# x's first piece loaded as two transfers of 64 rows instead of one of 128

## The chip, the core and the metric

The kernel runs on one core of a Trainium2 chip. The metric is device time in microseconds (us), the median of several runs. A profile is one execution of the same program, recorded by the chip's own profiler; its span goes from the first to the last recorded instruction, and is a little shorter than the device time.

The core has engines that run at the same time, each with its own instruction list: VectorE (DVE), ScalarE (ACT), GpSimd (POOL), TensorE (not used here) and SyncE (SP), which here only issues transfers and waits. Transfers between the chip's main memory (HBM) and the core's working memory (SBUF, 128 partitions) are carried by 16 DMA engines. SP and ACT can each issue transfers; each has its own queue, and both queues feed the same 16 DMA engines.

## What is computed

```python
def setup_inputs():
    batch, dim = 1024, 4096
    return {
        "x": np.random.randn(batch, dim).astype(np.float32),
        "y": np.random.randn(batch, dim).astype(np.float32),
    }

def reference(x: np.ndarray, y: np.ndarray) -> np.ndarray:
    z = x * y
    return (0.5 * z * (1 + np.tanh(np.sqrt(2 / np.pi) * (z + 0.044715 * z ** 3)))).astype(np.float32)
```

Two arrays of 16.78 MB are read, multiplied element by element, passed through the tanh form of GELU, and one array of 16.78 MB is written: 50.33 MB in all.

## The kernel before

Every element stands alone, so the kernel may lay the data out as it likes. It treats each array as flat, 32,768 elements for each of the 128 partitions, and cuts it into three pieces (`PIECES`, line 14). In the text they are called 0, 1 and 2:

- piece 0: columns 0 to 1,280; a row of one partition is 5,120 bytes, the whole piece 0.66 MB;
- piece 1: columns 1,280 to 17,664; a row is 65,536 bytes, the piece 8.39 MB;
- piece 2: columns 17,664 to 32,768; a row is 60,416 bytes, the piece 7.73 MB.

`columns` (line 51) makes the view of a piece: each partition's row is one contiguous run in HBM. All of x stays in SBUF (`xs`, line 61), and is overwritten by the product and then by the result. y has a smaller buffer (`ys`, line 62), parts of which are used twice. `Y_LOADS` (line 16) gives the order in which y's pieces are loaded and where in `ys` they go: piece 1, then piece 2, then piece 0. In the text these three transfers are y0, y1 and y2, the loads of x's pieces are x0, x1 and x2, and the stores, in the order of `STORES` (line 21), are those of piece 1, piece 2 and piece 0.

There is no scheduler: the program is written out by hand, and each engine works through its own list in order.

SP's list (lines 79 to 86 and 111 to 121): issue x0; take part in two barriers of all engines at the entry; wait until x0 has landed (line 81); issue y0 and x2; wait for three multiplies and issue y1; wait for the fourth and issue y2 (`Y_FREE`, line 18, gives these counts, since y1 and y2 reuse parts of y0's buffer); wait for y1's landing and issue the first store; wait for ACT and issue the second and the third store; wait until the stores have landed.

ACT's list: issue x1, the barriers, load the table of the GELU function, and then one ACTIVATE for each multiply as soon as that is done (lines 105 to 108).

DVE's list (lines 91 to 104): for each piece of y wait for the x piece with the same columns (lines 92 to 94) and for the y piece (line 95), then multiply in steps (`STEPS`, line 20): four of 4,096 columns, then seven of 2,048 and one of 768, then one of 1,280.

`_hoist` (line 25) takes instructions out of the place where they were written and puts them, in their order, ahead of their engine's first drain in the program's first block, that is, ahead of the entry barriers. Lines 79 and 80 do this with x0's issue on SP and x1's on ACT.

A transfer adds 16 to its semaphore in all, in single steps as the 16 DMA engines finish their share; so a wait for 16 is a wait until it has landed.

Of the kernel before, what the change touches and what calls it, by code (L numbers as in the profile page):

```python
# [1 line left out]

# [4 lines left out]


F32 = mybir.dt.float32
GELU = mybir.ActivationFunctionType.Gelu_apprx_tanh  # L10

PIECES = [(0, 1280), (1280, 17664), (17664, 32768)]

Y_LOADS = [(1280, 17664, 4056), (17664, 32768, 0), (0, 1280, 15104)]

Y_FREE = [0, 3, 4]

STEPS = [[4096] * 4, [2048] * 7 + [768], [1280]]  # L20
STORES = [(1280, 17664), (17664, 32768), (0, 1280)]
Y_BUF = 20440


def _hoist(nc, issued):

    here = nc.cur_bb.bb.instructions
    first = nc.main_func.blocks[0].instructions
    for ins in issued:
        del here[next(k for k, i in enumerate(here) if i is ins or i.name == ins.name)]  # L30
    engine = issued[0].engine
    at = next(
        k
        for k, i in enumerate(first)
        if i.engine == engine and type(i).__name__ == "InstDrain"
    )
    first[at:at] = issued


@with_exitstack  # L40
def kernel(
    ctx: ExitStack,
    tc: tile.TileContext,
    x: bass.AP,
    y: bass.AP,
    out: bass.AP,
):
    nc = tc.nc
    P = nc.NUM_PARTITIONS

    def columns(t, a, b):

        flat = t.flatten_outer_dims().rearrange("r c -> (r c)")
        pa, pb = next(q for q in PIECES if q[0] <= a and b <= q[1])
        return flat[P * pa : P * pb].rearrange("(p c) -> p c", p=P)[:, a - pa : b - pa]


    tc.close()
    tc.compile()  # L59

    xs = nc.alloc_sbuf_tensor("xs", [P, PIECES[-1][1]], F32).ap()
    ys = nc.alloc_sbuf_tensor("ys", [P, Y_BUF], F32).ap()
    sem_x = [nc.alloc_semaphore(f"sem_x{i}") for i in range(len(PIECES))]
    sem_y = [nc.alloc_semaphore(f"sem_y{i}") for i in range(len(Y_LOADS))]
    sem_mul = nc.alloc_semaphore("sem_mul")
    sem_act = nc.alloc_semaphore("sem_act")
    sem_o = [nc.alloc_semaphore(f"sem_o{i}") for i in range(len(STORES))]

    def load_x(i, engine=nc.sync):
        a, b = PIECES[i]  # L70
        return engine.dma_start(out=xs[:, a:b], in_=columns(x, a, b)).then_inc(sem_x[i], 16)

    def load_y(i):
        a, b, r = Y_LOADS[i]
        return nc.sync.dma_start(
            out=ys[:, r : r + b - a], in_=columns(y, a, b)
        ).then_inc(sem_y[i], 16)

    _hoist(nc, [load_x(0).ins])
    _hoist(nc, [load_x(1, nc.scalar).ins])  # L80
    nc.sync.wait_ge(sem_x[0], 16)
    load_y(0)
    load_x(2)
    for i in range(1, len(Y_LOADS)):
        if Y_FREE[i]:
            nc.sync.wait_ge(sem_mul, Y_FREE[i])
        load_y(i)

    n = 0
    done = {}  # L90
    for i, (a, b, r) in enumerate(Y_LOADS):
        for j, (xa, xb) in enumerate(PIECES):
            if xa <= a < xb:
                nc.vector.wait_ge(sem_x[j], 16)
        nc.vector.wait_ge(sem_y[i], 16)  # L95
        c = a
        for w in STEPS[i]:
            nc.vector.tensor_mul(  # L98
                out=xs[:, c : c + w],
                in0=xs[:, c : c + w],  # L100
                in1=ys[:, r + c - a : r + c - a + w],
            ).then_inc(sem_mul, 1)
            n += 1
            done[c + w] = n
            nc.scalar.wait_ge(sem_mul, n)
            nc.scalar.activation(  # L106
                out=xs[:, c : c + w], in_=xs[:, c : c + w], func=GELU
            ).then_inc(sem_act, 1)
            c += w

    for i, (a, b) in enumerate(STORES):
        if i == 0:
            nc.sync.wait_ge(sem_y[-2], 16)
        nc.sync.wait_ge(sem_act, done[b])
        nc.sync.dma_start(out=columns(out, a, b), in_=xs[:, a:b]).then_inc(sem_o[i], 16)
    for i in range(len(STORES) - 1):
        nc.sync.wait_ge(sem_o[i], 16)
    nums = sorted(s.num for s in [*sem_x, *sem_y, *sem_o[:-1], sem_mul, sem_act])
    assert nums == list(range(nums[0], nums[-1] + 1))
    nc.sync.sem_clear(range(nums[0], nums[-1] + 1))  # L120
    nc.sync.wait_ge(sem_o[-1], 16).then_inc(sem_o[-1], -16)


# [1 line left out]
_INS = ['x', 'y']  # L125
_OUTS = [((1024, 4096), 'float32')]


# [23 lines left out]
```

## Time and profile before

Three runs took 119.91, 119.82 and 119.84 us, a median of 119.84. The profiled execution's span is 118.52 us.

| from the profile before | us |
|---|---|
| device time, median of three runs | 119.84 |
| span of the profiled execution | 118.52 |
| x0 (on SP's queue): issued, landed | 0.00, 13.6 |
| x1 (on ACT's queue): issued, landed | 0.13, about 30.5 |
| y0: issued, landed | 13.57, 42.56 |
| x2: issued, landed | 13.96, about 60.4 |
| y1: issued, landed | 55.78, 78.25 |
| y2: issued, landed | 60.12, about 79.8 |
| store of piece 1: issued, landed | 78.27, about 98.7 |
| store of piece 2: issued | 96.55 |
| store of piece 0: issued, landed | 97.71, 118.5 |
| DVE busy in all, ACT busy in all | 35.2, 31.0 |

How to read it. "Issued" is the start of the issuing instruction on its engine, "landed" the time at which its semaphore was complete. A queue is worked off in order on each DMA engine, and a transfer issued behind another on the same queue starts only when the other's rows are done: x2's 46.5 us from issue to landing are mostly time behind y0. The trace also keeps a record for each packet that the DMA engines moved, with its start, duration and size, but without the number of the DMA engine; here a packet is one partition's row, and each transfer ends with one packet of 4 bytes on each DMA engine, its write to the semaphore. Where the text below gives times of rows or of semaphore writes, they are from these records. In the profile's lines SPq and ACTq stand for the issuing side of SP and ACT, and L71 is line 71 of the kernel.

### The profile page before, as it was taken

Reading aid. Unit: us, or ns where it says so; the run is one execution under the profiler, and the core shown is the slowest. Engines: PE = TensorE matmul, PEld = TensorE weight load, DVE = VectorE, ACT = ScalarE, POOL = GpSimd, SP = SyncE. Lnnn points to the kernel's source line nnn. Section 1 sums busy time; section 2 is a strip of 40 time slices with the busy share of each in tenths; the row PEclk is TensorE's granted clock in tenths of the full one; section 3 lists DMA queues with packets and bytes.
Section 4 is the critical chain, followed back from the end, with each engine's and each line's share of the span. In section 5 each row is a group of like instructions: output and inputs, shape, how many; then the busy total and the mean of one; then the engine's idle time right before and its main releaser. Section 6 shows DMA issues by size and latency. Waiting matters only on the chain.

```text
span 118.5 us, 82 instructions
## 1 busy us (share of the span) xinstructions
DVE 35.2 (30%) x13; ACT 31.0 (26%) x14; POOL 0.2 (0%) x4
## 2 busy tenths in 40 slices
DVE  0000000000000069999920000059999940000000
ACT  4000000000000000977975000006998990000000
POOL 0000000000000000000000000000000000000000
DMA  9888899889988897797797797798899887977975
GB/s 492 382 382 382 354 575 487 354 354 398 664 354 354 354 652 326 326 652 326 326 632 347 326 632 347 326 575 354 354 531 531 354 354 326 652 326 326 652 326 221
DMA packets 1296, 50.33 MB, mean 425 GB/s; under 512 B 144, under 2 KB 144, under 8 KB 528
## 3 DMA queue, kind: packets, MB, share of 16 engines
q1 hardware_dynamic: 1152, 41.94, 82.2%
q10 hardware_dynamic: 144, 8.39, 16.5%
HBM read 33.55 MB, written 16.78 MB: 425 GB/s over the span
## 4 chain that ended last, share of the span: by engine, by line
DMA 55%; DVE 24%; ACT 3%; issue 1%; DVEq 0%
DMA ys<-in_y_dram 43%; DVE xs L98 24%; DMA xs<-in_x_dram 11%; ACT xs L106 3%; DVEq L95 0%
## 5 line engine op out<-in xcount | busy, mean ns | idle before, releaser
L98 DVE TENSOR_TENSOR xs<-xs,ys 128x2048 f32<-128x2048 f32 (+3 forms) x13 | 35.2, 2777 | 60.9 <-DMA ys<-in_y_dram 60.9
L106 ACT ACTIVATE xs<-xs 128x2048 f32<-128x2048 f32 (+3 forms) x13 | 29.7, 2301 | 65.1 <-DVE xs L98 65.1
L106 ACT ACT_TABLE_LOAD x1 | 1.3, 1283 | 1.6 <-PEq L59 1.6
L136 POOL MEMSET const-bfloat16-1.0<- 128x1 bf16 x1 | 0.1, 103 | 0.0
L136 POOL MEMSET const-uint8-127<- 128x1 uint8 x1 | 0.1, 102 | 0.0
L136 POOL MEMSET const-float32-0.0<- 128x1 f32 x1 | 0.1, 100 | 0.2 <-issue 0.2
L136 POOL MEMSET const-float32-1.0<- 128x1 f32 x1 | 0.1, 99 | 0.0
## 6 DMA issues: line engine op xcount, KB each, us to landing
xs<-in_x_dram SPq DMA_DIRECT2D x1, 7552.0 KB, 46.5
ys<-in_y_dram SPq DMA_DIRECT2D x1, 7552.0 KB, 22.5
out_dram<-xs SPq DMA_DIRECT2D x1, 7552.0 KB, 20.4
xs<-in_x_dram SPq DMA_DIRECT2D x1, 640.0 KB, 13.6
ys<-in_y_dram SPq DMA_DIRECT2D x1, 640.0 KB, 19.7
out_dram<-xs SPq DMA_DIRECT2D x1, 640.0 KB, 20.8
xs<-in_x_dram ACTq DMA_DIRECT2D x1, 30.4
ys<-in_y_dram SPq DMA_DIRECT2D x1, 29.0
```

The costliest lines, as they stand in the source:

```text
L98: nc.vector.tensor_mul(out=xs[:, c : c + w], in0=xs[:, c : c + w], in1=ys[:, r + c - a : r + c - a + w],).then_inc(sem_mul, 1)
L106: nc.scalar.activation(out=xs[:, c : c + w], in_=xs[:, c : c + w], func=GELU).then_inc(sem_act, 1)
L136: nc = _bacc.Bacc("TRN2", target_bir_lowering=False, num_devices=1)
```

## The change

The load of x's piece 0 is made of two transfers, of partitions 0 to 63 and of partitions 64 to 127. Both are issued by SP, one behind the other, and both are hoisted ahead of the entry barriers, where the one transfer was. Each adds 16 to the same semaphore, so that the two places that wait for piece 0, SP ahead of y0's issue and DVE ahead of its last multiply, wait for 32. The bytes, their places in HBM and SBUF, and everything else stay as they were.

```diff
-    def load_x(i, engine=nc.sync):
+    def load_x(i, engine=nc.sync, p=slice(0, P)):
         a, b = PIECES[i]
-        return engine.dma_start(out=xs[:, a:b], in_=columns(x, a, b)).then_inc(sem_x[i], 16)
+        return engine.dma_start(out=xs[p, a:b], in_=columns(x, a, b)[p]).then_inc(sem_x[i], 16)
 
     def load_y(i):
...
-    _hoist(nc, [load_x(0).ins])
+    low, high = slice(0, P // 2), slice(P // 2, P)
+    _hoist(nc, [load_x(0, nc.sync, low).ins, load_x(0, nc.sync, high).ins])
     _hoist(nc, [load_x(1, nc.scalar).ins])
-    nc.sync.wait_ge(sem_x[0], 16)
+    nc.sync.wait_ge(sem_x[0], 32)
     load_y(0)
     load_x(2)
...
         for j, (xa, xb) in enumerate(PIECES):
             if xa <= a < xb:
-                nc.vector.wait_ge(sem_x[j], 16)
+                nc.vector.wait_ge(sem_x[j], 32 if j == 0 else 16)
         nc.vector.wait_ge(sem_y[i], 16)
```

## The prediction

> **What bounds the kernel now.** I began with the page of the profile: which engine is busy, and how evenly the transfers fill the span.
>
> ```profile
> span 118.5 us, 82 instructions
> DVE 35.2 (30%) x13; ACT 31.0 (26%) x14; POOL 0.2 (0%) x4
> DMA  9888899889988897797797797798899887977975
> DMA packets 1296, 50.33 MB, mean 425 GB/s; under 512 B 144, under 2 KB 144, under 8 KB 528
> q1 hardware_dynamic: 1152, 41.94, 82.2%
> q10 hardware_dynamic: 144, 8.39, 16.5%
> ```
>
> No compute engine works a third of the span, while the two DMA queues together hold the 16 DMA engines for 82.2 + 16.5 = 98.7% of it. Next, the table of stretches, to see where the missing 1.3% lies (columns: stretch, length, DVE, ACT, POOL, clock, DMA share, GB/s).
>
> ```profile
> 0.00:1.00 1.00, 0.00 (x0) 0.00 (x0) 0.20 (x4) 1.00 0.00 0
> 1.00:118.20 117.20, 35.20 (x13) 31.01 (x14) 0.00 (x0) 1.00 1.00 429
> 118.20:118.50 0.30, 0.00 (x0) 0.00 (x0) 0.00 (x0) 1.00 0.00 0
> ```
>
> It lies at the two ends. From 1.0 to 118.2 us the DMA share is 1.00: nothing can start earlier in the middle, so the end moves only with the work of the DMA engines, with a hole in their stream, or with its start. Then the timeline and SP's waits, for the order of the transfers.
>
> ```profile
> 0.00 0.38 SPq L71 DMA_DIRECT2D xs<-in_x_dram  x1
> 0.13 0.37 ACTq L71 DMA_DIRECT2D xs<-in_x_dram  x1
> ...
> 1.57 1.28 ACT L106 ACT_TABLE_LOAD   x1 [1.57 <-PEq L59]
> 13.57 0.34 SPq L75 DMA_DIRECT2D ys<-in_y_dram  x1
> 13.96 0.43 SPq L71 DMA_DIRECT2D xs<-in_x_dram  x1
> ```
>
> ```profile
> SPq L75 <- DMA xs<-in_x_dram: 12.0, 1, 12.0
> ```
>
> The 0.66 MB of x's first piece (x0) take until 13.57 us, because ACT's queue loads x1 beside it. In the packet records of the trace each DMA engine serves eight x0 rows (5,120 B, 196 ns), and from 2.3 us takes x1 rows (65,536 B, 2,418 ns) and x0's items in turn: five x0 rows before its first x1 row, then x1, row, x1, row, x1, row, x1, semaphore write. Check: 2.30 + 4 x 2.42 + 3 x 0.196 = 12.6 us; the semaphore writes stand at 12.66 to 13.19, and SP goes on 0.38 us after the last. x1's other four rows keep the engine busy until y0 arrives.
>
> **One engine's sum.** x0, y2 and the last store are 24 rows at 196 ns (4.7 us); x1 and the other two transfers of that width 24 rows at 2.42 us (58.1); the other three large ones 24 rows at 2.23 us (53.5): 116.3 us. The last engine starts its first row at 1.61 us, the first at 1.01; 1.61 + 116.3 = 117.9, against its last semaphore write at 118.11 and the end at 118.52. So the start of the last engine, and what its first rows lose, reach the end one for one. The median of the runs, 119.84, lies 1.32 us above this span; I add 1.32 to each span below.
>
> **The change, part by part.** *Second issue on SP.* One more instruction of 0.33 to 0.43 us (the issue rows of L75 and L71), at 0.38 us. Queued behind it: SP's part in the entry barriers. Its drain stands at 0.43 us, and the barrier passes when ACT's drain ends at 0.68; SP's now ends near 0.95, so the barriers pass some 0.3 us later, and with them the table load (1.57 to about 1.85). That is covered: the first ACTIVATE starts at 47.12 us, DVE waits for y0 until 42.66, SP for x0 until 13.57. Without cover it would cost 0.4 us. x1's issue is on ACT's own queue and is not moved.
>
> *Semaphores.* 16 more semaphore writes, one on each DMA engine, of 9 ns: 0.01 us. But each takes a turn against x1, so x0's ten items (4 rows, write, 4 rows, write) land at least one x1 packet, 2.4 us, later. The wait for 32 holds y0 and x2 back behind it on SP. The cover is x1: eight rows per engine. If n of the ten items are served before the first x1 row, the last write follows 10 - n x1 rows. With n = 5 (five fit before): 2.3 + 5 x 2.42 + 4 x 0.2 = 15.2 us. With n = 3: 2.3 + 7 x 2.42 + 5 x 0.39 = 21.2, some 21.7 on the last engine; y0's issue near 22.1 and its first packet 0.84 us later (the first large store: issued 78.27, first packet 79.11), 22.9, while the eighth x1 row still runs to 23.6. No hole, and y0's landing is set by bytes, not by its issue. DVE's wait for x0, at 94 us, has room to spare. What a later y0 would push: y1's issue at 55.78 waits for three multiplies behind y0, x2's transfer ends at 60.46; since a late stream delays both together, that margin stays.
>
> *64 rows instead of 128.* I take it that each half is still spread over all 16 engines, four rows each, as the 128 rows are; but it fills only half of SBUF's partitions at a time. The trace shows no such transfer, so bounds. Lower: rows keep their 196 ns, cost 0. A gain is possible at the start: the engines begin x0 spread over 0.60 us, and a list half as long may reach them in half the time, -0.3; at the very most all start with the first, -0.6. Upper: if two engines that fill the same half hold each other up so that together they move what one does, eight rows take 392 ns each: +8 x 0.196 = +1.57.
>
> Which end? Every long kind of packet runs at one rate per engine, 65,536 / 2,418 = 60,416 / 2,232 = 27.1 GB/s, loads and stores, beside rows of other transfers and without. That looks like a ceiling of the path into SBUF, not of HBM, and such a path can be shared. The nearest row of packets in one another's way is the first round: its 16 x1 rows, served while others still took x0 rows, averaged 2,544 ns, later ones 2,419. I take the upper end, less what waiting hides: five rows took 1.28 us at the start instead of 5 x 0.196 = 0.98, so 0.30 of it runs under that wait; and less half of the 0.3 gain. Sum: +1.57 - 0.30 - 0.15 = +1.12.
>
> The Trainium skill speaks against this part. "SBUF — State Buffer", section "Door 1: The DMA port swizzle", says that partitions 0 to 63 reach only 8 of 16 ports and so about 218 GB/s instead of 436; "DMA: Bandwidth & Descriptors", "Rules for kernel authors", says to use one transfer of 128 partitions instead of two of 64. By these figures, an estimate, x0's 0.66 MB would take 3.0 us instead of 1.5, +1.5 us; by the row alone (196 ns in every steady round) nothing. No run here shows it yet.
>
> **Forecast (A), 43%: the halves run at half rate, y0 still arrives in time.** 118.52 + 1.12 = 119.64 of span, 120.96 us. Its own range 120.2 to 121.6.
>
> **Rival B, 20%: slower still, a hole behind x1.** Place: 22 to 25 us. If ACT's x1 rows reach the engines earlier, since the load ahead of them is half as long, or the x0 rows are slow, only n = 2 items go first and the last write comes behind the eighth x1 row. Then all 16 engines stand still for SP's 0.38 and the issue's 0.84, 1.2 us, plus some spread. It decides from n = 2 on a single engine, as SP waits for the last. For it: at n = 3 the margin is only 0.7 us. Against: five rows went first before. Price 1.12 + 1.3 = 2.4: 122.3 us.
>
> **Rival C, 22%: nothing.** Rows keep 196 ns whatever half they fill; the later x0 is hidden behind x1's rows, as the full stream suggests: 119.84. For it: in the rounds from 7 us on, x0 and x1 rows mix at 196 and 2,419 ns without loss. Against: those rows all belong to transfers over 128 partitions.
>
> **Rival D, 15%: faster.** Row rates hold, and the shorter first list ends the 0.60 us spread sooner: -0.3, 119.5 us; the limit of -0.6 gives 119.2. Against: at 79.1 us ten idle engines got the first packets of a 128-row store within 0.09 us, so the length of a list hardly makes the spread there.
>
> That the change does not do what it says would need one half to be issued behind a barrier; SP's second issue then stands well after 0.4 us, and x0 lands later, with C's or B's time.
>
> **From cases to numbers.** 120.96 is A's. A measurement of this kernel (119.82 to 119.91) can tell about 0.2%, 0.24 us, from no change. Faster: D, 0.15. Same: nearly all of C, 0.21. Slower: A, B and C's edge, 0.64. The range, 119.5 to 122.4, takes in A, C and most of B; it leaves out most of D and the end of B with the bound 1.57 + 1.4, some 0.18.
>
> **What will show it.** Packets 1,312 instead of 1,296 and two x0 issues near 0.0 and 0.4 us: the change as described. x0 rows near 390 ns outside the first ones, and y0's landing at 43.7 instead of 42.56: A. y0's issue at 15 to 22 us with a DMA share of 1.00 around 20 to 25: hidden; a stretch there with a share well under 1: B. Rows at 196 ns and y0's landing unmoved: C. First x0 packets closer together and all landings earlier: D. I am wrong if the later x0 moves the end with no hole and no slow rows, or if time is lost behind 60 us.

## The result, and the profile after

The changed kernel takes 125.3 us (median of four runs, 124.94 to 125.56) against 119.83 of the kernel before: a ratio of 1.045, with a 95% interval of 1.043 to 1.047. The profiled execution's span is 124.2 us against 118.5. It was forecast slower, at 120.96 us and at most 122.4; the loss is five times the forecast one.

First the page of the kernel after: the span, the DMA engines' share in 40 slices, and the queues.

```profile
span 124.2 us, 83 instructions
...
DMA  9999979998779978979789797799977997797975
...
DMA packets 1312, 50.33 MB, mean 405 GB/s; under 512 B 160, under 2 KB 160, under 8 KB 544
q1 hardware_dynamic: 1168, 41.94, 79.0%
q10 hardware_dynamic: 144, 8.39, 17.9%
```

1,312 packets: the change is as described, with 16 more semaphore writes and the same bytes. The queues now hold the DMA engines for 79.0 + 17.9 = 96.9% of the span instead of 98.7, so about 3.9 us are empty instead of 1.5. And x1's queue, q10, moves its 8.39 MB in 17.9% of 124.2 = 22.2 us of engine time instead of 16.5% of 118.5 = 19.6: the same rows have become slower.

The stretches of the kernel after say where (length, DVE, ACT, POOL, clock, DMA share, GB/s):

```profile
1.00:24.50 23.50, 0.00 (x0) 1.28 (x1) 0.00 (x0) 1.00 1.00 378
24.50:25.80 1.30, 0.00 (x0) 0.00 (x0) 0.00 (x0) 1.00 0.45 126
25.80:27.40 1.60, 0.00 (x0) 0.00 (x0) 0.00 (x0) 1.00 0.00 0
27.40:123.90 96.50, 35.21 (x13) 29.73 (x13) 0.00 (x0) 1.00 1.00 428
```

There is a hole: nothing moves between 25.8 and 27.4 us, and the stretch before it is half empty. Ahead of the hole the share is 1.00 at only 378 GB/s: engines that are busy and slow. Behind it, the stream runs to the end as it did before. So the whole loss lies ahead of the hole, in the hole and in the first rows after it, whose packets are longer.

The timeline of the kernel after names the order, and three lines of its chain of work that ended last give the first issue by itself and x0's landing:

```profile
0.00 1.19 SPq L71 DMA_DIRECT2D xs<-in_x_dram  x2
0.12 0.38 ACTq L71 DMA_DIRECT2D xs<-in_x_dram  x1
...
26.50 0.34 SPq L75 DMA_DIRECT2D ys<-in_y_dram  x1
26.90 0.42 SPq L71 DMA_DIRECT2D xs<-in_x_dram  x1
```

```profile
0.00 0.56 SPq L71
...
0.61 25.88 DMA xs<-in_x_dram
...
26.50 21.74 DMA ys<-in_y_dram
```

SP's two issues take 1.19 us together; by themselves, 0.556 and 0.578 us, where the one issue of 128 rows took 0.383. So x1's issue, which starts at 0.12, is finished at 0.505 us, before the first half's at 0.556. Before, x0's was finished first (0.383 against x1's 0.494). And the packet records show x1's rows first: the 16 DMA engines start one x1 row each at 1.14 to 1.67 us, the first x0 row comes at 4.15, and from then on each engine takes x0's ten items and x1's rows in turn. x0 lands behind all eight x1 rows: its last semaphore write starts at 25.72, SP issues y0 at 26.50, and y0's first row starts at 27.48.

The sum over the packet records, as a mean over the 16 DMA engines:

| us per DMA engine | before | after | more |
|---|---|---|---|
| from 1.0 us to the first row of all | 0.01 | 0.14 | 0.13 |
| idle from the first row on | 0.38 | 2.57 | 2.19 |
| x1's rows, over 2,418 ns each | 0.16 | 2.84 | 2.68 |
| y0's rows, over 2,418 ns each | 0.01 | 0.69 | 0.68 |
| x0's rows, over 196 ns each | 0.30 | 0.34 | 0.04 |
| together | | | 5.72 |

The end of the last semaphore write moved by 5.68 us, so the table closes within 0.04. Below, "idle time" is its second row. Of x1's 2.68 us, 0.57 are its first rows, which now open the stream (3,117 ns on average, 2,544 before); about 2.1 come from six rounds in which an x0 row was served beside an x1 row (2,718 to 2,838 ns on average). In the one round that had only the first half's semaphore writes beside it, x1's rows took 2,422 ns.

### The profile page after: what moved, and what is told of

The parts are those of the page before. It is cut to its first block, busy times and chain, and to the rows that moved or that the text cites. A ratio compares the mean times of both kernels' runs of the same rounds, so it can differ in the third digit from the quotient of the medians.

```text
span 124.2 us, 83 instructions
## 1 busy us (share of the span) xinstructions
DVE 35.2 (28%) x13; ACT 31.0 (25%) x14; POOL 0.2 (0%) x4
## 2 busy tenths in 40 slices
DMA packets 1312, 50.33 MB, mean 405 GB/s; under 512 B 160, under 2 KB 160, under 8 KB 544
## 3 DMA queue, kind: packets, MB, share of 16 engines
q10 hardware_dynamic: 144, 8.39, 17.9%
## 4 chain that ended last, share of the span: by engine, by line
DMA 56%; DVE 22%; ACT 3%; issue 1%; SPq 0%; DVEq 0%
DMA ys<-in_y_dram 36%; DVE xs L99 22%; DMA xs<-in_x_dram 21%; ACT xs L107 3%; SPq L71 0%; DVEq L96 0%
```

## The experiments

Two theories came out of this. **Order:** which of the first two issues is finished first decides whose rows go first; the loser pays with x0's landing behind x1, the hole and slow first rows. **Half:** rows of 16 DMA engines into one half of SBUF's partitions hold up the other transfer. The rival to both, **Turns**: the second transfer's own items are the cost. Each run is compared with the kernel before on the same chip (119.84 to 119.92 us).

**x1's issue later, the halves unchanged (`a_x1drain`).** It moves one issue by 0.08 us.

```diff
-def _hoist(nc, issued):
+def _hoist(nc, issued, behind=0):
...
-    first[at:at] = issued
+    first[at + behind : at + behind] = issued
...
-    _hoist(nc, [load_x(1, nc.scalar).ins])
+    _hoist(nc, [load_x(1, nc.scalar).ins], 1)
```

> The changed kernel, with x1's issue on ACT put behind ACT's first drain instead of ahead of it, so some 0.15 us later. Order (x1's list was complete at 0.50 us, the first half's at 0.56, and the DMA engines take what is complete first): now the first half of x0 is first by about 0.1 us; first x0 row near 1.2 us and ahead of the first x1 row, x0 landed near 15 to 18 us instead of 26.5, y0 issued before 20 us, no hole, about 121.3 to 122.3 us with the slow x1 rows left. If the order is not set by which issue ends first: 125.3, x1 rows still first.

121.51 us, ratio 1.016 (1.012 to 1.021). Its timeline:

```profile
0.00 1.18 SPq L71 DMA_DIRECT2D xs<-in_x_dram  x2
0.20 0.37 ACTq L71 DMA_DIRECT2D xs<-in_x_dram  x1
...
20.14 0.35 SPq L75 DMA_DIRECT2D ys<-in_y_dram  x1
```

x1's issue now ends at 0.569 us, 17 ns behind the first half's 0.552. That is enough: x0's rows start at 1.34 us, all four of the first half go ahead of the first x1 row at 2.57, and y0 is issued at 20.14, just after the forecast 20, and in time. The idle time is 0.39 us, as in the kernel before, though the first row starts 0.33 us later. So 3.8 of the 5.5 us hung on 0.08 us of one issue. Of the 1.6 us that are left, 0.9 are Half: x1's rows beside the second half's rows took 215 to 224 ns more in each of four rounds. The rest is the later first row, x1's first rows (2,784 ns instead of 2,544) and x0's.

**x0 whole, but behind x1 (`b_x0late`).** The kernel before with x0's issue behind the barriers.

```diff
-    _hoist(nc, [load_x(0).ins])
+    load_x(0)
```

> The kernel before, x0 in one transfer of 128 rows, but issued behind the entry barriers, so that x1 comes first. Order: x0's nine items go one by one between x1's rows, x0 lands near 22 to 24 us behind x1's rows, a hole of 1.5 to 2.3 us and a slow restart of 0.66, 122.3 to 123 us; x1 rows beside x0 rows stay at 2,418 ns. Half (only transfers of 64 partitions cost): 119.8 us. Turns (the second transfer's semaphore writes cost): 119.8 us.

122.75 us, ratio 1.025 (1.023 to 1.027): Order alone, without a second transfer and without halves.

```profile
0.13 0.36 ACTq L71 DMA_DIRECT2D xs<-in_x_dram  x1
...
1.56 0.38 SPq L71 DMA_DIRECT2D xs<-in_x_dram  x1
...
23.55 0.33 SPq L75 DMA_DIRECT2D ys<-in_y_dram  x1
```

SP issues x0 at 1.56 and y0 at 23.55 us; the idle time is 2.17 us, and y0's first rows take 3,149 ns instead of 2,418. x1's rows beside x0's rows stay at 2,418 to 2,420 ns: a turn of 128-partition rows slows nobody.

**Without the wait (`a_nowait`, `b_nowait`).** SP issues y0 without waiting for x0, in both kernels; the line that goes has 16 instead of 32 in the kernel before.

```diff
-    nc.sync.wait_ge(sem_x[0], 32)
```

> The changed kernel without SP's wait for x0 ahead of y0's issue (y0 goes to its own buffer, the wait only orders). Accounting of the two traces: the hole (2.2 us) and the slow restart of y0 (0.66) go, the slow x1 rows (2.7) stay: 122.4 us. If the hole only shows time lost elsewhere: 125.3 us.

> The kernel before without SP's wait for x0, as the control of the run above. No hole to take away: 119.8 us, within 0.3; if the wait itself buys something in the kernel before, more.

The changed kernel comes to 122.61 us, ratio 1.021 (1.016 to 1.026, without the longest run), the kernel before to 119.80, ratio 0.9997 (0.9987 to 1.0006). The hole is gone (idle 0.40 us), the slow x1 rows stay, as forecast. The slow restart does not go whole: y0's first rows took 2,789 ns, after 3,101 in the changed kernel. The scatter of this run is large, 121.85 to 123.80 us, and the trace is of the longest, in which x1's rows lost 3.4 us. So it supports the split of the 5.5 us into two roughly equal parts, 2.5 to 3.0 us each, for the hole with what follows and for slow rows, and no finer. In the kernel before, the wait costs nothing.

**Even and odd partitions (`x0_evenodd`).** Still two transfers of 64 rows.

```diff
-    low, high = slice(0, P // 2), slice(P // 2, P)
+    low, high = slice(0, P, 2), slice(1, P, 2)
```

> The changed kernel with its two transfers of 64 rows made of the even and of the odd partitions instead of the lower and the upper 64. Half (rows of all 16 DMA engines into one half of SBUF get in the way of x1's rows): x1 rows beside x0 rows go back to about 2,420 ns; if the issue still takes 0.56 us, x1 is still first and x0 still lands behind it, so a hole and a slow restart are left: about 122.7 us, as for x0 in one transfer behind x1. If any transfer of 64 rows slows its neighbours: 125.3 us and x1 rows of 2,700 to 2,900 ns.

122.66 us, ratio 1.023 (1.021 to 1.025). The two issues take 0.545 and 0.578 us, x1 is first, and the hole is there:

```profile
1.00:22.40 21.40, 0.00 (x0) 1.28 (x1) 0.00 (x0) 1.00 1.00 416
22.70:24.50 1.80, 0.00 (x0) 0.00 (x0) 0.00 (x0) 1.00 0.05 20
24.50:121.00 96.50, 35.21 (x13) 29.73 (x13) 0.00 (x0) 1.00 1.00 428
```

These are the stretches of this kernel, columns as above. Ahead of the hole 416 GB/s move instead of 378, and x1's rows beside x0's rows took 2,418 ns in every round. The same number of rows, items and issues, other partitions, and 2.6 us less: that is Half, shown by itself. It also shows that 64 rows are not slow as such. One thing is not separated: with the partitions, the rows' places in HBM change too (every second row instead of 64 in a run). That the cost arises at SBUF's partitions and not in HBM is argued, not shown, by these runs.

**Halves by columns (`x0_colhalves`).** Two transfers over all 128 partitions, 640 columns each.

```diff
-    def load_x(i, engine=nc.sync, p=slice(0, P)):
+    def load_x(i, engine=nc.sync, c=slice(None)):
         a, b = PIECES[i]
-        return engine.dma_start(out=xs[p, a:b], in_=columns(x, a, b)[p]).then_inc(sem_x[i], 16)
+        return engine.dma_start(out=xs[:, a:b][:, c], in_=columns(x, a, b)[:, c]).then_inc(sem_x[i], 16)
...
-    low, high = slice(0, P // 2), slice(P // 2, P)
+    low, high = slice(0, 640), slice(640, 1280)
```

> x0 as two transfers of 128 rows and 640 columns (2,560 bytes a row), both on SP ahead of the barriers, waits for 32. Order: an issue of 128 rows ends at 0.38 us, so x0's rows are first again. Turns: 16 rows and two semaphore writes for each DMA engine; if some 6 to 9 of the 18 go ahead of x1, 9 to 12 turns are left for eight x1 rows, x0 lands behind x1, hole and restart: about 122.5 us, with x1 rows at 2,420 ns. If the number of items did not matter: 119.9 us.

122.42 us, ratio 1.021 (1.019 to 1.022). The first issue takes 0.386 us, x0 is first, and its eight rows go ahead of x1. But the first half's semaphore write and the second half's nine items then take their turns against x1's eight rows, x0 lands behind them (last write 23.4 us), and the hole is back (idle 2.50 us). So Turns is a cost too, where the items outnumber x1's rows; the number of rows in a transfer matters here more than its bytes.

**Halves where nothing runs beside them (`b_y2halves`, `b_y1halves`).** The kernel before, with one load of y as two transfers of lower and upper partitions; the second run has `i == 1`, with the waits to match.

```diff
+        if i == 2:
+            for p in (slice(0, P // 2), slice(P // 2, P)):
+                nc.sync.dma_start(
+                    out=ys[p, r : r + b - a], in_=columns(y, a, b)[p]
+                ).then_inc(sem_y[i], 16)
+            return
...
-        nc.vector.wait_ge(sem_y[i], 16)
+        nc.vector.wait_ge(sem_y[i], 32 if i == 2 else 16)
```

> The kernel before with y2 (5,120-byte rows as x0) as two transfers of 64 rows, lower and upper partitions, in a place where nothing runs beside it and where the order can't change. Half: its eight rows for each DMA engine take about 392 ns instead of 196, +1.57 us, 121.4 us. If halves cost only beside another transfer: 119.9 us. Its issues show what a 64-row issue takes alone: 0.56 us, or 0.33 if the 0.56 came from ACT's issue beside it.

> The kernel before with y1 (60,416-byte rows, 7.73 MB) as two transfers of 64 rows, lower and upper partitions: the rate of such a transfer over a long time. Half at full strength: rows of 4,460 ns instead of 2,230, +17.8 us, 137.7 us. If the loss is only in the meeting of different rows: 119.9 us.

With y2: 121.24 us, ratio 1.011 (1.010 to 1.013), +1.3 us; its rows took 321 ns on average, up to 398, instead of 196. With y1, in a single run: 139.86 us, +19.9. Two lines from the chain that ended last in the run with y1:

```profile
55.81 0.52 SPq L77
...
56.38 41.88 DMA ys<-in_y_dram
```

y1 lands 41.9 us after its second issue; before, 22.47 us after its one issue. Its rows took 4,692 ns behind the first 16, against 2,230. The halves thus run at slightly less than half rate, also without a neighbour. Both runs issue 64 rows in 0.52 to 0.59 us at a quiet time, so the long issue belongs to the 64 rows and not to ACT's issue beside it.

**How sharp the order is (`b_x0drain`, `b_x1drain`).** The kernel before with x0's issue, or x1's, put behind its engine's drain, by the `behind=1` of above.

> The kernel before, one transfer of 128 rows, with x0's issue behind SP's first drain instead of ahead of it. A test of how sharp the order is: the start of x0's issue moves by the length of the drain, and x1's issue still ends near 0.50 us. Order: if x0's issue ends after x1's, x1 rows go first and the time is 122.4 to 123.0 us; if it still ends before, x0 rows go first and the time is 119.9 us. Whichever it is must agree with the two ends in the trace; a mixture that does not would speak against the order theory.

> The kernel before with x1's issue behind ACT's first drain: the control for the run of the halves with x1 later. Order: x0 is first in both, so 119.9 us, within 0.3; more lead for x0 (all eight rows first instead of five) lets it land earlier than 13.6 us, which buys nothing, as the end is set by bytes.

`b_x1drain`: 119.82 us, ratio 0.9999 (0.9990 to 1.0009). All eight x0 rows go first, y0 is issued at 6.01 us instead of 13.57, and the end does not move. `b_x0drain`: 121.8 us, ratio 1.015 (1.011 to 1.019), neither of the two times that the expectation named.

```profile
0.08 0.38 SPq L71 DMA_DIRECT2D xs<-in_x_dram  x1
0.13 0.37 ACTq L71 DMA_DIRECT2D xs<-in_x_dram  x1
...
21.23 0.33 SPq L75 DMA_DIRECT2D ys<-in_y_dram  x1
```

x0's issue still ends first (0.457 against 0.499 us) and its rows still go first, and yet it costs 2.0 us. The records fit two x0 rows ahead of the first x1 row on every DMA engine, instead of five: x0's 16 semaphore writes start together, at 20.27 to 20.85 us, where the turns put them behind seven x1 rows. y0's first rows, at 22.69, then come just as the last x1 rows end, and took 2,935 ns. The engines came apart: y0's semaphore writes are spread over 1.62 us instead of 0.52. Engines that are done early wait later for the first store, which needs y1 whole: between 79.5 and 81 us, 0.8 us for each engine are idle, against 0.1 around 79 us in the kernel before. With one transfer, the lead thus goes with the number of x0 rows ahead: eight at 0.19 us (`b_x1drain`), five at 0.11, two at 0.04. It is not the whole rule, as with halves four rows went ahead at 0.02 (`a_x1drain`). What sets the number is left open.

**Both mended (`evenodd_x1drain`).** Even and odd partitions, with x1's issue behind ACT's drain: the changes of `x0_evenodd` and `a_x1drain` together.

> Both mended at once: x0 as even and odd partitions, and x1's issue behind ACT's drain so that x0's first half is first. If order and halves of SBUF are the whole cost: x1 rows at 2,420 ns, y0 issued before 20 us, no hole; what is left is the later first row (a 64-row issue ends at 0.56 us instead of 0.38), 0.2 to 0.4 us: 120.0 to 120.3 us. If a third cost sits in the second transfer: above 120.8 us.

120.27 us, ratio 1.004 (1.003 to 1.006): y0 is issued at 19.08 us, x1's rows from the second round on take about 2,420 ns, and there is no hole. So the two causes account for all but 0.4 us of the 5.5; the rest fits the first x0 row, at 1.33 instead of 1.01 us. Two transfers of 64 rows, even with both causes out of the way, gain nothing over one of 128.

## Why the prediction was wrong, point by point

**What bounds the kernel** was read rightly: the stream of the DMA engines from 1.0 us on, in which the start and any hole reach the end one for one. Both losses lie there, and nothing was lost behind y0's first rows, which end near 31 us.

**The step that failed: "*Second issue on SP.* One more instruction of 0.33 to 0.43 us".** The price was taken from rows that all issue 128 partitions. The 64-row issues took 0.556 and 0.578. As work on SP that is as well covered as the text said: the barriers passed about 0.9 us later, where the text had 0.3, and the table load, at 2.50 us, still had 49 us to spare. But the text asked only who waits behind SP. It did not ask against whom the issue runs: x1's, which before ended 0.11 us behind x0's. "x1's issue is on ACT's own queue and is not moved" was true, and was taken for harmless.

**The number of items served first** followed from that. The text counted with n = 5 and n = 3, and rival B with n = 2; it was 0. Rival B's mechanism (eight x1 rows as the cover, SP's release and the issue behind it) is what happened, and it had 20%; the place was 24.5 to 27.4 us instead of 22 to 25. Its price of 1.3 us for the hole was too small: 2.19 us of idle time, and, without a term in the text, 0.68 for y0's slow first rows and 0.57 for x1's. SP's release took 0.79 us after the last semaphore write, where the text had 0.38. In `a_x1drain`, also with lower and upper partitions, it took 0.59; in all other runs with the wait, 0.32 to 0.41.

**64 rows instead of 128** was the right mechanism. The Trainium skill's rule from "SBUF — State Buffer", "Door 1: The DMA port swizzle", that partitions 0 to 63 reach only 8 of 16 ports, agrees with the long run: 4,692 ns a row instead of 2,230. Even and odd partitions, which by that section's map reach all ports, lost nothing. The size was off for this place: +1.12 was forecast, and the lower and upper partitions cost 2.6 us (`x0_evenodd` against the changed kernel). The bound of +1.57 is near the 1.3 measured where halves run alone. Beside x1, the rows that lost were not x0's, which took 226 ns on average and not 390, but x1's, by 300 to 420 ns in a round, where the bound has 196; with x1 later it was 215 to 224. Why the meeting costs more in the one order than in the other is open.

**Rivals C and D** are out: the rows do not keep their rate, and the first packets came no sooner (1.14 us, and x1's). D's argument, that a list half as long starts sooner, was the wrong way round: its issue is longer.

**The same loss by parts.** x1 first costs 2.7 to 2.9 us (`x0_evenodd`, `b_x0late`), lower and upper partitions instead of even and odd 2.6. Together 5.3 to 5.5, against 5.5 measured. The parts depend on which is taken first: with x1 later, the order is worth 3.8 us (`a_x1drain`), the partitions then 1.2 (`evenodd_x1drain`), and 0.4 are left.

## What to carry to other kernels

Where two queues start together, look at which issue ends first and by how much: a lead of 0.1 us decided here whether a small transfer went ahead of a large one or crept along between its rows, one row a turn, until the large one was done. Price a changed issue by its own form, and ask who races it, not only who waits behind it. Cut a transfer so that each part still covers partitions of the whole range; the lower and the upper 64 run at half rate and slow their neighbours too.

## What the runs showed of the hardware that was not expected

- An issue of 64 rows took 0.52 to 0.59 us in every place, one of 128 rows 0.33 to 0.46, for the same row length (5,120 and 60,416 bytes). The exception is x2's issue right behind y0's in three runs: 4.08 us (`a_x1drain`), 4.21 (`evenodd_x1drain`) and 2.69 (`b_x0drain`). Its cause is open; x2's rows come behind y0's in any case.
- The first rows of a 65,536-byte transfer on an idle stream took about 0.7 us longer than the next ones: x1's at 1.14 us (+0.70) and y0's at 27.48 us (+0.68) in the changed kernel. In the kernel before, where x0's small rows open the stream, x0's and x1's rows lost 0.46 us together.
- Of two transfers in one another's way, the slow rows can be those of the transfer that was not changed: x0's rows took 226 ns beside x1, x1's up to 2,838 instead of 2,418.
- A semaphore write takes a turn of its own between the queues: a round with nothing but that write still cost x0 a whole x1 row.
